# Three-branch attention with two more buffers and a longer pipeline, and the low part of softplus on VectorE

## Chip, cores and metric

The kernel runs on one core of a Trainium2 chip, as one program with one launch. The metric is the device time of that program in microseconds (us); lower is better. The median of three runs of the kernel before is 2275.87 us (2273.51 to 2281.44).

## What is computed

Two transformer blocks for one sequence of 512 tokens with 1024 channels. The first block has a hybrid mixer, a cross attention and a feed-forward part. The second has two layers. Its first layer is stick-breaking attention, its second is an attention with three branches, and each is followed by an MLP. Every weight matrix product is made three times, as high times high, low times high and high times low part, to keep float32 accuracy. The two places that the change touches are these, shortened from the reference:

```python
# stick-breaking attention, 16 heads of 64
z = einsum('bqhd,bshd->bhqs', q, k) * scale
causal = key_pos[None, :] < t[:, None]
log_1m = where(causal, log_sigmoid(-z), 0.0)          # -softplus(z)
excl = cumsum(log_1m, axis=3, reverse=True) - log_1m
a = where(causal, exp(log_sigmoid(z) + excl), 0.0)
o = einsum('bhqs,bshd->bqhd', a, v)

# attention with three branches: compressed keys, selected blocks, window; 16 heads in 4 groups
p_cmp = softmax(where(valid_c, q . k_cmp * scale, NEG))
p_sel = softmax(where(valid_s, q_rot . k_sel * scale, NEG))
p_w   = softmax(where(valid_w, q_rot . k_w * scale, NEG))
out   = sum over the branches of gate * (p @ v), then @ w_o
```

At 512 tokens the 8 key blocks are fewer than the 16 that would be selected, and the window holds all 512 tokens, so the second and third branch are both plain causal attention, with keys and values of their own.

## The kernel before

The program goes through seven stages (`PHASES`): mixer, cross attention, feed-forward, stick-breaking attention, MLP, three-branch attention, MLP. Weights stream in from HBM piece by piece. `Weights.hi` makes the high part of a piece on ScalarE (line 341) and `Weights.lo` its low part, tile `wl`, on VectorE (line 350). The program is scheduled by hand: each engine does its instructions in the order in which the Python code records them, and waits where one of them needs what is not there yet. So the two tables below set the work of every engine in the two stages.

**Stick-breaking attention** (`s_all`). The unit is a head, 16 in all. A step of the loop over `i` records the parts of `S_ORDER`, each for the unit that is its lag behind. Part `proj` makes the projection of a pair of heads (in even steps the queries, in odd steps the keys), 24 matmuls. `scores` makes z in PSUM. `evac` (tile `st`, line 1614) is the scaled copy of the projection. `cap` limits z to 30 into tile `sT` (lines 1662 and 1663, two instructions). `exp` makes Exp and Ln on ScalarE (1668, 1669), `soft` takes the maximum with z (1675, 1676). `high` runs on GpSimd: two small instructions and the high part `sph` of the softplus (1684, 1685, 1686). `low` is the difference `spl` of the softplus and its high part (1691), 128 x 1280, also on GpSimd. `weights` then adds the sums of both parts to the scores on TensorE. It has a lag of 1, so it stands behind the projection and the scores of the next unit. `low` has lag 1 as well and stands behind `scores` and ahead of `evac` and `cap` in the table.

**Three-branch attention** (`n_attend`). The work is cut into 4 groups of heads. A group has one unit for the compressed branch, called c unit below (methods `c_...`), and then 32 units (methods `n_...`): two pairs of heads, for each pair both other branches (b = 0 and 1), for each the two heads, and for each head four blocks of 128 queries in the order 3, 2, 0, 1, where block c has c + 1 blocks of keys. There are 132 units in all. The table `ORDER` says which part is recorded for which unit in iteration `i`: part with lag L works on unit i - L.

```python
ORDER = (("scores", 0), ("out", 7), ("head", 9), ("bias", 1), ("turn", 4), ("exp", 2),
         ("sums", 2), ("tick", 0), ("move", 5), ("scale", 2))
```

`scores` (TensorE) writes one of three PSUM banks. `bias` (VectorE, line 2055) adds the causal mask, scales and finds the row extreme, into a buffer `np` of which there are `NP`. `exp` (ScalarE, 2060) also sums the rows. `sums` (VectorE, 2064) takes the reciprocal. `scale` (GpSimd, 2069) multiplies by it and by the gate. `turn` (TensorE, 2077) transposes the probabilities into one of four PSUM banks. `move` copies them to SBUF, half on VectorE (2088), half on ScalarE (2090). `out` (TensorE) does the product with the values only after the last block of the second head of a pair, so in every eighth unit, with 16 matmuls. Where b is 0 four more go ahead of them, for the compressed branch (tile `cp`). `head` splits a finished pair of heads. For a c unit the same parts do more: `c_bias` has three VectorE instructions of 128 x 512, `c_sums` four, and `c_scale` (2162) one on GpSimd.

`tick` records one more instruction of each background generator. Here it is `g_query`, which rotates the queries of the next pair of heads: a shuffle on VectorE, six instructions on GpSimd, and then for each head a high part on ScalarE (2034), a low part on VectorE (2036) and a DMA of the result to the other half of the partitions (2039, tile `nq`). It is started in iteration 4 and 20 of a group (`QSTART`), and so its second, eighth and following instructions come in fixed iterations after that. `DRAIN` places the first matmuls of the output projection in the last iterations.

Of the kernel before, what the change touches and what calls it, by code (L numbers as in the profile page):

```python
# [10 lines left out]
F32 = mybir.dt.float32  # L11
# [3 lines left out]
ALU = mybir.AluOpType  # L15
# [15 lines left out]
PHASES = ("mix", "xattn", "ffn", "stick", "mlp1", "nsa", "mlp2")  # L31
BANKS = {"b": range(8), "bp": [0], "bo": [1], "za": [2, 3], "zb": [4, 6],
         "s": [0, 1, 2], "t": [3, 4, 5, 6], "av": [7], "f": [0, 1, 2, 3]}
NP = 6
FF_BLOCKS = ((0, 8), (8, 16), (16, 22))
SHUF = list(range(8, 16)) + list(range(0, 8)) + list(range(16, 32))

# [430 lines left out]
class Kernel:  # L468
# [1219 lines left out]

    def s_low(self, i):
        t, _, hi, lo, _, _ = self.hd[i]  # L1690
        self.nc.gpsimd.tensor_tensor(lo, t, hi.bitcast(F32), op=ALU.subtract)  # L1691

    def s_weights(self, i):

# [250 lines left out]
    def gate(self, gt):  # L1945
# [3 lines left out]
        for c in range(4):  # L1949
# [9 lines left out]

    QORD = (3, 2, 0, 1)  # L1960

    ORDER = (("scores", 0), ("out", 7), ("head", 9), ("bias", 1), ("turn", 4), ("exp", 2),
             ("sums", 2), ("tick", 0), ("move", 5), ("scale", 2))
    DRAIN, QSTART = 9, 4

    def n_attend(self):
        self.causal = self.wide("causal", self.ph, "causal")
# [17 lines left out]

        for i in range(n + max(lag for _, lag in self.ORDER) + 1):
            if i == n:
                lead = [(self.W.get(f"no{m}", 3 - m), self.bank("s")) for m in range(3)]
            for part, lag in self.ORDER:
                if part == "tick":  # L1990
# [11 lines left out]
        nxt, nx = self.next_norm() if self.nxt else None, self.newx() if self.nxt else None  # L2002
        self.back, self.fetched, self.back_tag = {}, 0, ("np", NP)
        self.fetch(2)
# [45 lines left out]
    def n_bias(self, u):  # L2050

        w = P * u["c"] + P
        p = u["p"] = self.tmp("np", bufs=NP)[:, :w]
        u["mx"] = self.tmp("nmx", (P, 1), bufs=8)
# [77 lines left out]
    def c_bias(self, u):  # L2132
        nc = self.nc
        p = u["p"] = self.tmp("np", bufs=NP)
        mask = self.cst("cmp_mask").rearrange("p (c n) -> p c n", c=4)
# [68 lines left out]
```

## Time and profile before

| what | value |
|---|---|
| median of three runs | 2275.87 us |
| the profiled execution | 2278.95 us |
| its span, first to last instruction | 2277.1 us |
| mean granted TensorE clock | 0.980 of full |
| TensorE busy | 2159.2 us (95%) |
| VectorE, ScalarE, GpSimd busy | 1230.7, 870.4, 494.5 us |
| stick-breaking units with `weights` waiting for GpSimd | 961 to 1128 us of the span |
| three-branch units | 1683 to 1863 us of the span |

TensorE is busy nearly all the time, and most of it is weight products back to back. The two stages of the change are the ones in which TensorE waits in a repeating pattern. They are read with the waits by engine, the timelines by engine, and busy time in stretches. A share of busy time over the whole span says little here.

### The profile page before, as it was taken

The numbers are of one execution on the slowest core, as the hardware profiler recorded it, in microseconds if no ns is written. First come the engines' busy times: TensorE is split into PE (matmuls) and PEld (weight loads), VectorE is DVE, ScalarE is ACT, GpSimd is POOL, SyncE is SP. The second block draws the span as 40 slices with busy tenths as digits, with TensorE's granted clock in tenths as the row PEclk, the third lists the DMA queues.
The fourth block names the chain that finished last, engine by engine and source line by source line (L and its number), as shares of the span: only waits on it lengthen the run. The fifth ranks groups of instructions, "written<-read, shape, count | busy, mean of one in ns | idle before, by whom it ended". The sixth has DMA issues, their size and how long they took to land.

```text
span 2277.1 us, 26704 instructions
## 1 busy us (share of the span) xinstructions
PE 2159.2 (95%) x10250; PEld 1750.3 (77%) x10250; DVE 1230.7 (54%) x1917; ACT 870.4 (38%) x1377; POOL 494.5 (22%) x495
## 2 busy tenths in 40 slices
PE   8899999999999999999899999998988889999998
PEld 5677788888888887777678888887775568888886
DVE  6998756454333435666545443446567755534333
ACT  4333434343222224355534232232446653523222
POOL 3333401111110104244410000023447651000001
PEclk9999999999999999999999999999999999999999
DMA  4122434122323222422133332332330113332231
GB/s 142 61 70 71 133 108 152 57 73 93 102 93 102 92 85 92 130 65 65 47 120 94 101 102 93 100 107 99 118 95 20 30 43 116 93 102 93 93 102 65
DMA packets 63376, 205.94 MB, mean 90 GB/s; under 512 B 7952, under 2 KB 8336, under 8 KB 63120
## 3 DMA queue, kind: packets, MB, share of 16 engines
q1 hardware_dynamic: 59504, 196.86, 27.6%
q10 hardware_dynamic: 3744, 7.37, 0.9%
q8 instruction: 80, 1.31, 0.2%
q14 instruction: 48, 0.39, 0.1%
HBM read 189.39 MB, written 6.29 MB: 86 GB/s over the span
## 4 chain that ended last, share of the span: by engine, by line
PE 74%; DVE 12%; POOL 5%; issue 4%; ACT 4%; DMA 0%; ACTq 0%; POOLq 0%; DVEq 0%; SPq 0%
PE psum L540 59%; PE b L540 12%; DVE wl L350 2%; PE psum L2077 1%; POOL spl L1691 1%; DVE t L908 1%; DVE pv L1089 1%; POOL np L2069 1%; POOL sph L1686 1%; POOL cx L1802 1%; DVE xl L553 1%; ACT xh L552 1%; ACT sT L1668 0%; ACT sT L1669 0%; DVE prev L1061 0%
## 5 line engine op out<-in xcount | busy, mean ns | idle before, releaser
L540 PE MATMUL psum<-xh,wh 128*128 128x512 f32 x1560 | 611.4, 392 | 1.0 <-DVE h L628 0.9
L540 PE MATMUL psum<-xh,wl 128*128 128x512 f32 x1560 | 608.6, 390 | 1.8 <-DVE wl L350 1.5
L540 PE MATMUL psum<-xl,wh 128*128 128x512 f32 x1560 | 608.5, 390 | 0.0
L341 ACT ACTIVATE wh<-ws 128x1024 fp32r<-128x1024 f32 (+1 forms) x346 | 356.3, 1038 | 388.9 <-PE psum L540 327.9
L350 DVE TENSOR_TENSOR wl<-ws,wh 128x1024 fp32r<-128x1024 f32 (+2 forms) x332 | 427.0, 1291 | 105.5 <-ACT wh L341 105.2
L540 PEld LDWEIGHTS psum<-xh,wl 128*128 128x128 f32 x1560 | 293.0, 188 | 66.1 <-DVE wl L350 4.3
L540 PEld LDWEIGHTS psum<-xh,wh 128*128 128x128 f32 x1560 | 293.3, 188 | 63.1 <-issue 3.0
L540 PEld LDWEIGHTS psum<-xl,wh 128*128 128x128 f32 x1560 | 293.3, 188 | 61.0 <-DVE xl L550 0.3
L540 PE MATMUL b<-xh,wh 128*128 128x512 f32 (+1 forms) x488 | 195.0, 400 | 8.5 <-ACT wh L341 6.7
L540 PE MATMUL b<-xh,wl 128*128 128x512 f32 (+1 forms) x488 | 192.6, 395 | 3.8 <-POOL wl L350 1.9
L540 PE MATMUL b<-xl,wh 128*128 128x512 f32 (+1 forms) x488 | 192.4, 394 | 0.5 <-DVE xl L553 0.5
L540 PE MATMUL psum<-hh,wh 128*128 128x512 f32 x320 | 125.1, 391 | 0.0
L540 PE MATMUL psum<-hh,wl 128*128 128x512 f32 x320 | 124.6, 389 | 0.0
L540 PE MATMUL psum<-hl,wh 128*128 128x512 f32 x320 | 124.6, 389 | 0.0
L1357 DVE TENSOR_TENSOR h<-h,psum 128x512 f32<-128x512 f32 x48 | 33.1, 689 | 161.2 <-PE psum L540 161.2
L540 PEld LDWEIGHTS b<-xh,wh 128*128 128x128 f32 (+1 forms) x488 | 92.5, 189 | 28.4 <-ACT wh L341 6.7
L1348 ACT ACTIVATE t<-t 128x512 f32<-128x512 f32 x64 | 40.5, 632 | 188.9 <-DVE t L1347 188.9
L540 PEld LDWEIGHTS b<-xh,wl 128*128 128x128 f32 (+1 forms) x488 | 92.0, 188 | 26.3 <-DVE wl L350 3.3
L553 DVE SCALAR_TENSOR_TENSOR xl<-h,cols,xh 128x512 fp32r<-128x512 f32 x64 | 76.6, 1213 | 61.8 <-ACT xh L552 61.8
L540 PEld LDWEIGHTS b<-xl,wh 128*128 128x128 f32 (+1 forms) x488 | 92.4, 189 | 20.4 <-DVE xl L553 1.2
L2069 POOL TENSOR_SCALAR np<-np,nsm,gates 128x512 f32<-128x512 f32 (+3 forms) x128 | 83.4, 654 | 46.8 <-DVE nsm L2064 34.1
L2077 PE MATMUL psum<-small,np 128*128 128x128 f32 x336 | 66.4, 302 | 27.2 <-POOL np L2069 19.1
(497 smaller groups left out, 3159.3 us busy)
## 6 DMA issues: line engine op xcount, KB each, us to landing
ws<-in_wst SPq DMA_DIRECT2D x332, 512.0 KB, 3.4
h<-in_xT SPq DMA_DIRECT2D x16, 256.0 KB, 3.7
kk<-kk SPq DMA_DIRECT2D x16, 256.0 KB, 3.3
nq<-nq SPq DMA_DIRECT2D x16, 256.0 KB, 2.9
ws<-in_wst SPq DMA_DIRECT2D x8, 384.0 KB, 3.1
spill<-back SPq DMA_DIRECT2D x8, 256.0 KB, 2.0
back<-spill ACTq DMA_DIRECT2D x8, 256.0 KB, 3.6
spill<-h ACTq DMA_DIRECT2D x8, 256.0 KB, 5.8
```

Of the source, the lines that this page charges most:

```text
L341: self.nc.scalar.activation(hi[:, :n], s, AF.Copy)
L350: e.tensor_tensor(lo[:, :n], s, hi[:, :n].bitcast(F32), op=ALU.subtract)
L540: self.nc.tensor.matmul(ps, a, b, start=start, stop=stop, skip_group_check=again)
L552: nc.scalar.activation(hi, src, AF.Copy, scale=scale)
L553: nc.vector.scalar_tensor_tensor(lo, src, scale, hi.bitcast(F32), op0=ALU.mult, op1=ALU.subtract)
L908: nc.vector.scalar_tensor_tensor(t, u[:, q:q + T], cw[:, q:q + 1], t, op0=ALU.mult, op1=ALU.add)
L1089: nc.vector.tensor_tensor(o[:, a:], src[:, a:], src[:, a - n:528 - n], op=ALU.add)
L1348: nc.scalar.activation(t, t, AF.Square)
L1357: nc.vector.tensor_tensor(self.h[:, m, :], self.h[:, m, :], ps, op=ALU.add)
L1686: self.nc.gpsimd.tensor_scalar(hi, t, 1.0, 0.0, op0=ALU.mult, op1=ALU.add)
L2069: self.nc.gpsimd.tensor_scalar(u["p"], u["p"], u.pop("sm"), self.gates[:, u["c"], e:e + 1], op0=ALU.mult, op1=ALU.mult)
L2077: self.nc.tensor.transpose(ps[:, s], p[:, s], self.ident)
```

## The change

Three edits. The low part of softplus is recorded on VectorE instead of GpSimd, at the same place of the stage's table. The buffers `np` go from 6 to 8. The table of the three-branch attention gets longer lags (turn 4 to 6, move 5 to 7, out 7 to 9, head 9 to 10, scale 2 to 4, sums 2 to 3) and another order within an iteration: `scale` right behind `sums`, `head` behind it, `tick` last. `DRAIN` follows.

```diff
-NP = 6
+NP = 8
...
     def s_low(self, i):
         t, _, hi, lo, _, _ = self.hd[i]
-        self.nc.gpsimd.tensor_tensor(lo, t, hi.bitcast(F32), op=ALU.subtract)
+        self.nc.vector.tensor_tensor(lo, t, hi.bitcast(F32), op=ALU.subtract)
...
-    ORDER = (("scores", 0), ("out", 7), ("head", 9), ("bias", 1), ("turn", 4), ("exp", 2),
-             ("sums", 2), ("tick", 0), ("move", 5), ("scale", 2))
-    DRAIN, QSTART = 9, 4
+    ORDER = (("scores", 0), ("out", 9), ("bias", 1), ("turn", 6), ("exp", 2), ("sums", 3),
+             ("scale", 4), ("head", 10), ("move", 7), ("tick", 0))
+    DRAIN, QSTART = 10, 4
```

How instructions stand on two engines, before and now. On VectorE, between two units of the stick-breaking stage (the number in a name counts tiles, `sT_6880` is the first unit's and `sT_6942` the second's):

```order
 L1676 TENSOR_TENSOR sT_6880<-sT_6880,psum 128x768
 L350 TENSOR_TENSOR wl_6899<-ws_6753,wh_6898 128x1024
+L1691 TENSOR_TENSOR spl_6894<-sT_6880,sph_6893 128x1280
 L1614 SCALAR_TENSOR_TENSOR st_6940<-psum,r_begin 128x512
 L1662 TENSOR_SCALAR sT_6942<-psum 128x512
```

The low part of one unit now stands in VectorE's queue ahead of the copy of the projection and the cap of the next unit. GpSimd's queue keeps the three instructions of `high` alone.

On TensorE, in the first group of the three-branch stage, where the second pair of heads begins. `nq_11664` is the second head of the first pair; the first head of the second pair is `nq_11848` before and `nq_11842` now; `cp` and `pt` are operands of `out`. Before:

```order
L540 MATMUL psum<-pt_11768,vs_10631 64x128
L540 MATMUL psum<-pt_11823,vs_10631 64x128
L2077 MATMUL psum<-small,np_11840 128x128
L540 MATMUL psum<-ks_10630,nq_11664 128x256 x2
L2077 MATMUL psum<-small,np_11854 128x128 x2
L540 MATMUL psum<-ks_10630,nq_11848 128x512 x2
L2077 MATMUL psum<-small,np_11869 128x128 x4
```

And now:

```order
L540 MATMUL psum<-ks_10630,nq_11664 128x256 x2
L2077 MATMUL psum<-small,np_11802 128x128 x4
L540 MATMUL psum<-ks_10630,nq_11664 128x256 x2
L2077 MATMUL psum<-small,np_11815 128x128 x3
L540 MATMUL psum<-ks_10630,nq_11842 128x512 x2
L540 MATMUL psum<-cp_11770,vc_11691 64x512 x2
L540 MATMUL psum<-pt_11785,vs_10631 64x512
```

Before, the long `out` was done two units ahead of the new head's first scores. Now it comes right behind them.

## Rows read from the trace of the kernel before

**Rows 1.** The page: busy time by engine; the chain that ended last, by engine.
```profile
PE 2159.2 (95%) x10250; PEld 1750.3 (77%) x10250; DVE 1230.7 (54%) x1917; ACT 870.4 (38%) x1377; POOL 494.5 (22%) x495
...
PE 74%; DVE 12%; POOL 5%; issue 4%; ACT 4%; DMA 0%; ACTq 0%; POOLq 0%; DVEq 0%; SPq 0%
```

**Rows 2.** Waits, stick-breaking stage (950 to 1145): waiter, releaser: total, times, longest.
```profile
PE psum L540 <- POOL spl L1691: 17.4, 9, 3.1
```

**Rows 3.** Timeline of TensorE, first matmul on spl: start, us, what [idle before].
```profile
964.74 0.69 PE L540 MATMUL psum<-spl,none 128*128 128x384 f32 x1 [2.91 <-POOL spl L1691]
987.82 0.44 PE L540 MATMUL psum<-spl,none 128*128 128x384 f32 x1 [1.83 <-POOL spl L1691]
1011.42 0.44 PE L540 MATMUL psum<-spl,none 128*128 128x384 f32 x1 [1.84 <-POOL spl L1691]
...
1127.73 0.44 PE L540 MATMUL psum<-spl,none 128*128 128x384 f32 x1 [3.15 <-POOL spl L1691]
```

**Rows 4.** Timeline of GpSimd, one pair of units, and spl of the first and 15th.
```profile
961.41 3.27 POOL L1691 TENSOR_TENSOR spl<-sT,sph 128x1280 fp32r<-128x1280 f32 x1
1006.24 2.13 POOL L1686 TENSOR_SCALAR sph<-sT 128x1280 fp32r<-128x1280 f32 x1
1008.45 2.91 POOL L1691 TENSOR_TENSOR spl<-sT,sph 128x1280 fp32r<-128x1280 f32 x1
1015.72 1.26 POOL L1686 TENSOR_SCALAR sph<-sT 128x1280 fp32r<-128x1280 f32 x1
1017.06 2.95 POOL L1691 TENSOR_TENSOR spl<-sT,sph 128x1280 fp32r<-128x1280 f32 x1
...
1123.94 3.73 POOL L1691 TENSOR_TENSOR spl<-sT,sph 128x1280 fp32r<-128x1280 f32 x1
```

**Rows 5.** Timeline of VectorE, the same pair of units, and a wl alone.
```profile
999.90 0.96 DVE L1663 TENSOR_SCALAR sT<-psum 128x768 f32<-128x768 f32 x1 [0.30 <-PE psum L540]
1005.70 1.53 DVE L350 TENSOR_TENSOR wl<-ws,wh 128x1024 fp32r<-128x1024 f32 x1 [0.58 <-ACT wh L341]
1007.75 0.69 DVE L1614 SCALAR_TENSOR_TENSOR st<-psum,r_begin 128x512 f32<-128x512 f32 x1 [0.51 <-PE psum L540]
1008.40 0.69 DVE L1662 TENSOR_SCALAR sT<-psum 128x512 f32<-128x512 f32 x1
...
1017.78 3.32 DVE L350 TENSOR_TENSOR wl<-ws,wh 128x1024 fp32r<-128x1024 f32 x1 [3.17 <-ACT wh L341]
...
1152.07 1.23 DVE L350 TENSOR_TENSOR wl<-ws,wh 128x1024 fp32r<-128x1024 f32 x1 [2.49 <-ACT wh L341]
```

**Rows 6.** Waits, three-branch stage (1690 to 1863), columns as in rows 2.
```profile
DVE nsm L2064 <- ACT np L2060: 21.6, 46, 1.9
...
PE psum L2077 <- POOL np L2069: 18.9, 34, 2.9
...
PE psum L2077 <- POOL np L2162: 7.9, 4, 2.2
```

**Rows 7.** Stretches: us, busy PE, PEld, DVE, ACT, POOL, granted clock, DMA.
```profile
1733.00:1755.00 22.00, 18.84 (x114) 13.04 (x114) 15.69 (x66) 15.35 (x46) 16.00 (x24) 0.92 0.11 25
1755.00:1777.00 22.00, 18.19 (x123) 12.79 (x122) 16.90 (x66) 14.33 (x43) 14.71 (x24) 1.00 0.12 27
```

**Rows 8.** Timeline of TensorE: turn of two c units; out of one pair and the next head.
```profile
1734.28 1.11 PE L2077 MATMUL psum<-small,np 128*128 128x128 f32 x4 [1.89 <-POOL np L2162]
...
1748.00 1.08 PE L540 MATMUL psum<-cp,vc 128*64 128x512 f32 x4
...
1751.70 0.71 PE L540 MATMUL psum<-ks,nq 128*128 128x512 f32 x2
...
1777.79 0.83 PE L2077 MATMUL psum<-small,np 128*128 128x128 f32 x4 [1.89 <-POOL np L2162]
```

**Rows 9.** VectorE's low part of that head; its DMA, from issue to landing.
```profile
1747.01 0.68 DVE L2036 TENSOR_TENSOR nq<-qr,nq 64x512 fp32r<-64x512 f32 x1
...
DMA to landing us min/median/max: 2.8/2.9/4.4
```

## The prediction

> **What bounds the kernel now.** The page comes first: TensorE is busy 95% of the span, and 74% of the chain that ended last lies on it [rows 1]. So only what TensorE waits for, or what makes it slower, can give time back. The waits by engine then say where it waits. In the stick-breaking stage it is one thing: nine waits for the low part `spl`, 17.4 us in all [rows 2]. Of these the first unit has 2.91 and the 15th 3.15 us, and the 11 us that are left are six waits like the two shown, 1.83 to 1.84 us, one in every pair of units [rows 3]. A pair takes 1011.42 - 987.82 = 23.6 us. In the three-branch stage TensorE waits for GpSimd's `scale`: 18.9 us in 34 waits on ordinary units and 7.9 us in four waits on c units, 26.8 us together [rows 6]. The c units stand 1777.79 - 1734.28 = 43.5 us apart, which is one group [rows 8].
>
> Is any engine full there? In 44 us of a group TensorE is busy 18.84 + 18.19 = 37.0 us, and VectorE 15.69 + 16.90 = 32.6 us [rows 7]. None is. TensorE's clock is 0.92 in one of the two stretches: 0.08 x 22 = 1.8 us of clock lost per group. The slow stretch begins behind a wait of 1.89 us for a c unit [rows 7, 8], so I count part of that loss to the waits. Without waits and at full clock TensorE would need 37.0 - 1.8 = 35.2 us per group. VectorE comes close behind it, with 32.6 / 33 = 0.99 us per unit. The stage is bound by the latency from one engine to the next, with two engines nearly full beneath it.
>
> **Term 1: low part on VectorE.** It removes 16 GpSimd instructions of 2.91 to 3.73 us [rows 4] and adds 16 on VectorE. No row shows that one there. The nearest are the same subtraction on 1024 columns, 1.23 us alone, and a 512-column instruction, 0.69 us [rows 5]. The slope gives 1.23 + 256 x 0.54 / 512 = 1.50 us for 1280. The upper bound is the same subtraction when disturbed: `wl` took 3.32 us when it began inside a GpSimd `spl` [rows 4, 5], so 3.32 x 1.25 = 4.1 us. I take 1.50, as GpSimd has nothing left to do behind `sph` until the next unit.
>
> The new wait is on VectorE. `spl` waits for `sph`, and behind it stand `st` and both caps of the next unit. That closes a loop that was not there: cap, Exp and Ln, maximum, `sph`, `spl`, `st`, cap of the next unit. From the second cap to the start of `spl` it is 1008.45 - 999.90 = 8.55 us [rows 4, 5]. Then `spl` 1.50, `st` 0.65 and the first cap 0.65 (start to start, 1008.40 - 1007.75): 11.35 us per unit, 22.7 per pair. Before it was 23.6, so a pair saves 0.9 us, and six pairs 5.4. What is late next is this loop, no longer GpSimd.
>
> In 8.55 `sph` counts at 2.13 us. The other unit of the pair had it at 1.26 [rows 4], with no `wl` beside it. With 1.26 there the pair would be 21.8 us, and TensorE's own work is 23.6 - 1.84 = 21.8, so a pair saves at most 1.8 and six 10.8. I take the smaller saving: the odd unit's chain now starts later, behind `spl`, and its `sph` comes to lie beside the `wl` of 1017.78. The Trainium skill (SBUF, section "Who interferes with whom") says that a VectorE instruction with two SBUF inputs and a GpSimd instruction that reads SBUF exclude each other for a whole instruction. The trace agrees: 3.32 is 1.23 plus about what was left of the running `spl`. By that rule both units stand at 2.13 and six pairs save 5.4; by the undisturbed row 10.8.
>
> The first unit's wait shrinks by 3.27 - 1.50 = 1.8 us, and the 15th's by 3.73 - 1.50 = 2.2. The DMAs of the keys come about 2 us later in a step and have a projection of 24 matmuls to hide behind: nothing. Term 1 is 5.4 + 1.8 + 2.2 = **9 us**, between 4 (the pairs gain nothing) and 15.
>
> **Term 2: the longer pipeline.** No instruction is added or removed. Before, the transposes of a unit follow its reciprocal by two iterations, and that reciprocal waits in the same iteration for Exp: 46 such waits on VectorE, 21.6 us [rows 6]. TensorE can thus be about one unit ahead of VectorE. When it comes to an `out` it leaves VectorE about one unit of work and then issues no scores for 2 to 3 us (an `out` with its `cp` begins at 1748.00, and the new head's scores, the second ones behind it, at 1751.70 [rows 8]). VectorE runs dry, and TensorE later waits for what VectorE did not do. Now the transposes follow the reciprocal by three iterations, and Exp has an iteration to itself. The lead grows to about two units, so each of the 16 `out`s costs one unit less: 16 x 0.99 = 15.8 us. Eight buffers are what the two extra iterations need: with six, bias would take a buffer in the iteration in which it is transposed. They do nothing else.
>
> For the c unit the compressed branch gets two iterations more, and an `out` now falls in its iteration. Of four waits (7.9 us) I leave 1 us each: 4 us gained, bounds 0 and 7.9.
>
> Against this stands a transfer. The low part of the next pair's first head comes in iteration 13, now at its end, and its scores in iteration 17. Before, the low part began at 1747.01 and the scores at 1751.70, with an `out` between; the DMA takes 2.9 us [rows 8, 9]. Now that `out` stands behind the scores. TensorE is one to two units ahead, so it arrives two units or one, 2.0 or 1.0 us, after the low part, and waits 1.0 to 2.0 us. I take 1.5 in each of four groups: 6 us lost, bounds 0 and 3.0 each, or 12. The even pairs have the c unit between and lose nothing.
>
> The clock: 1.8 us per group, 7 us in all. About half of the waits go, so I take half of that, 3.5.
>
> Term 2 is 15.8 + 4 - 6 + 3.5 = **17 us**, between a loss of 4 (half of the lead's gain, no other gain, 12 lost to the transfer) and (43.5 - 35.2) x 4 = 33 (TensorE never waits). A group should take about 39 us. The extra iteration at the end only drains, beside the output projection's first matmuls: nothing.
>
> **Sum.** 9.4 + 17.3 is 27 us. The profiled execution took 2278.95, so 2252; it lies 3.1 us above the median, so the median becomes 2275.87 - 27 = 2249 us.
>
> **Rivals.**
> - *The waits only move.* VectorE at 0.99 us per unit is close to TensorE, and the transfer waits its full 2.9 us. Then term 2 is 8 - 12 = -4, term 1 stays 9: 2271. For it speaks that the two engines are busy 37.0 and 32.6 of 44 us [rows 7]; against it that the 26.8 us of waits come from units whose chain gets two more iterations. Chance 0.08.
> - *Slower: `spl` disturbed on VectorE.* If it takes 4.1 us, the loop is 8.55 + 4.1 + 1.3 = 13.95 us and a pair 27.9: six pairs lose 25.8, first and 15th unit 1.2. With term 2 the time is 2275.87 + 27 - 17 = 2286. It decides from 11.8 - 9.85 = 1.95 us on. Against it: the disturbance in the rows needs a GpSimd instruction at the same time, and none is left there. Chance 0.04. The same section of the Trainium skill asks for such a partner too.
> - *TensorE becomes the only bound.* Both terms at their upper ends, 15 + 33: 2228. For it speaks that the new lags take every direct wait apart; against it the transfer and VectorE's 32.6 us. Chance 0.07.
> - *The change does not do what it says*, as the added buffers push something else: the order on the engines shows both moves, so 0.01.
>
> **How the numbers follow.** The forecast has 0.80, and its bounds are 4 - 4 and 15 + 33 us gained, both terms seldom at one end. The range from 2230 (46 us gained) to 2268 (8 us) leaves out those ends and with them the second rival and most of the first and third, under 0.2 in all. About 7 us, 0.3% of the time, is what a measurement of this kernel can tell from no change. Faster than 2269: forecast 0.80, third rival 0.07 and a part of the first, together 0.90. Within 0.3%: 0.06. Slower: 0.04.
>
> **What would show it.** Right: waits of TensorE on `spl` near 1 us per pair, now with VectorE as releaser, `spl` at 1.5 us, pairs 22.7 us apart; c units about 39 us apart; waits on `scale` below 15 us in all; a new TensorE wait of 1 to 2 us ahead of the third head's first scores in each group. Wrong: `spl` above 1.95 us, pairs at 23.6 us or more, or groups still at 43 us.

## The result and the profile after

| what | before | after |
|---|---|---|
| median | 2274.73 us (four runs, 2273.51 to 2281.44) | 2252.02 us (four runs, 2250.17 to 2254.06) |
| ratio, 95% interval | | 0.9894 [0.9872, 0.9917] |
| span of the profiled execution | 2277.1 us | 2250.8 us |
| mean granted TensorE clock | 0.980 | 0.986 |
| stick-breaking stage, with the weight product behind it | 233.70 us | 224.34 us |
| next stretch, up to the three-branch stage | 479.75 us | 475.33 us |
| three-branch stage | 260.85 us | 247.62 us |
| TensorE busy in the stick-breaking stage (1087 matmuls) | 212.44 us | 210.86 us |
| TensorE busy in the next stretch (some 2086 matmuls) | 467.51 us | 462.93 us |
| TensorE busy in the three-branch stage (1281 matmuls) | 230.03 us | 224.14 us |

The change is faster by 1.1% (0.8 to 1.3%), and 2252 lies 3 us above the forecast. By the ratio it gained 24 us, where 27 were forecast. The stages are cut at the same instruction in both traces. Term 1 came to 233.70 - 224.34 = 9.4 us (forecast 9.4), term 2 to 260.85 - 247.62 = 13.2 us (forecast 17.3). Of the 4.4 us of the stretch between them about 3.4 belong to one execution and not to the change; experiment 8 shows it.

What a stage lost is idle time of TensorE or busy time. Its matmuls are the same in both kernels, so less busy time for them goes with the granted clock. Term 1 is 7.8 us of idle time (21.3 to 13.5) and 1.6 us of busy time, at a clock of 0.98 before and 0.99 now. Term 2 is 7.3 us of idle time (30.8 to 23.5) and 5.9 us of busy time, at 0.94 and 0.97.

**The page of the changed kernel**, busy time by engine and the chain by engine [rows 1]:

```profile
PE 2148.9 (95%) x10250; PEld 1740.8 (77%) x10250; DVE 1228.7 (55%) x1933; ACT 864.4 (38%) x1377; POOL 449.0 (20%) x479
...
PE 71%; DVE 14%; ACT 5%; POOL 5%; issue 4%; DMA 1%; ACTq 0%; POOLq 0%; DVEq 0%; SPq 0%
```

Sixteen instructions went from GpSimd to VectorE, and yet VectorE is busy 2 us less than before (1228.0 us in experiment 1, where they alone moved): most of the 23.9 us it took over it got back from its own instructions beside GpSimd. From 940 to 1150 the mean `wl` went from 2.12 to 1.34 us, and the low parts of the keys (`kk`) from 17.9 to 9.5 us in all. Of the chain 3% has gone from TensorE and 2% to VectorE.

**Stick-breaking stage.** Waits of TensorE, 940 to 1145, columns as in [rows 2]:

```profile
PE psum L540 <- DVE spl L1691: 7.0, 9, 1.1
PE psum L540 <- POOL sph L1686: 2.4, 2, 1.3
PE psum L540 <- ACT sA L1717: 1.8, 2, 1.3
```

The 17.4 us of [rows 2] are now 7.0 us, with VectorE as releaser. The second and third line are partly new: 2.4 instead of 1.3, and 1.8 instead of nothing. Where the time came from is read from the first matmul on `spl` of each unit, on the timeline of TensorE [rows 3]:

```profile
963.73 0.69 PE L540 MATMUL psum<-spl,none 128*128 128x384 f32 x1 [1.08 <-DVE spl L1691]
...
985.79 0.45 PE L540 MATMUL psum<-spl,none 128*128 128x384 f32 x1 [1.09 <-DVE spl L1691]
...
1030.47 0.45 PE L540 MATMUL psum<-spl,none 128*128 128x384 f32 x1 [0.58 <-DVE spl L1691]
...
1052.83 0.45 PE L540 MATMUL psum<-spl,none 128*128 128x384 f32 x1 [0.58 <-DVE spl L1691]
...
1097.49 0.44 PE L540 MATMUL psum<-spl,none 128*128 128x384 f32 x1 [0.57 <-DVE spl L1691]
1108.02 0.44 PE L540 MATMUL psum<-spl,none 128*128 128x384 f32 x1 [1.09 <-DVE spl L1691]
1118.49 0.45 PE L540 MATMUL psum<-spl,none 128*128 128x384 f32 x1 [0.82 <-DVE spl L1691]
```

A pair takes 1052.83 - 1030.47 = 22.4 us; it was 23.6. TensorE still waits 0.57 us in each. The rest of a pair is then 21.8 us, TensorE's own work as worked out before. What it waits for is the new loop, and it stands whole on the chain of work that ended last (start, us, what), here for one unit:

```profile
1040.19 1.49 DVE spl L1691
1041.68 0.60 DVE st L1614
1042.28 0.60 DVE sT L1662
1042.88 0.88 DVE sT L1663
...
1043.84 1.28 ACT sT L1668
...
1045.15 1.28 ACT sT L1669
...
1047.06 0.96 DVE sT L1676
...
1049.12 2.14 POOL sph L1686
...
1051.28 0.81 DVE spl L1691
```

From one `spl` to the next it is 1051.28 - 1040.19 = 11.1 us; 11.35 was forecast. In [rows 4] one unit of a pair had `sph` at 2.13 us and the other at 1.26. Here are two units in a row, on GpSimd's timeline, and the `wl` beside them on VectorE's:

```profile
1049.12 2.13 POOL L1686 TENSOR_SCALAR sph<-sT 128x1280 fp32r<-128x1280 f32 x1
...
1060.20 2.30 POOL L1686 TENSOR_SCALAR sph<-sT 128x1280 fp32r<-128x1280 f32 x1
```

```profile
1048.58 1.53 DVE L350 TENSOR_TENSOR wl<-ws,wh 128x1024 fp32r<-128x1024 f32 x1 [0.58 <-ACT wh L341]
1051.28 1.49 DVE L1691 TENSOR_TENSOR spl<-sT,sph 128x1280 fp32r<-128x1280 f32 x1 [1.17 <-POOL sph L1686]
...
1060.15 1.22 DVE L350 TENSOR_TENSOR wl<-ws,wh 128x1024 fp32r<-128x1024 f32 x1 [1.07 <-ACT wh L341]
1062.54 1.49 DVE L1691 TENSOR_TENSOR spl<-sT,sph 128x1280 fp32r<-128x1280 f32 x1 [1.16 <-POOL sph L1686]
```

Both units are now disturbed by a `wl`. Take the second: `sph` begins at 1060.20 and `wl` runs until 1061.37, so 1.17 us of it are left; 1.26 + 1.17 = 2.43, and the row has 2.30. `spl` itself has 1.49 us in all 16 units, and `wl` no longer has its 3.32 us of [rows 5].

**Three-branch stage.** Waits of TensorE, 1670 to 1850 [rows 6], then of VectorE, and of VectorE in the kernel before (1690 to 1863):

```profile
PE psum L540 <- DVE nmx L2055: 8.6, 18, 1.3
PE psum L540 <- DMA nq<-nq: 6.3, 4, 1.6
PE psum L2077 <- POOL np L2069: 5.0, 8, 1.6
PE psum L2077 <- POOL np L2162: 1.1, 3, 0.4
```

```profile
DVE np L2055 <- PE psum L540: 17.7, 9, 3.0
DVE ol L550 <- ACT oh L549: 10.6, 7, 1.7
...
DVE nsm L2064 <- ACT np L2060: 1.6, 4, 0.4
```

```profile
DVE np L2055 <- PE psum L540: 10.7, 13, 2.0
DVE ol L550 <- ACT oh L549: 5.7, 4, 1.9
```

The waits on `scale` fell from 18.9 to 5.0 us, those on the c unit from 7.9 to 1.1, and the 46 waits of VectorE on Exp from 21.6 to 1.6. Two lines are new. TensorE's scores wait for `bias` (8.6 us; before it was a single wait of 1.4 us, at the start of the stage), and the third head of each of the four groups waits for its transfer (6.3 us). In all it is 21.0 us instead of 26.8 + 1.4 = 28.2. VectorE still runs dry at `out`: it has nine waits of up to 3.0 us on the scores, and seven in `head` (`ol`) on ScalarE, which needs the result of an `out`. So of the 20 us that it no longer waits for Exp, 12 have moved to these two lines (10.7 to 17.7 and 5.7 to 10.6). Start times on TensorE's timeline, of two late transfers [rows 8]:

```profile
1732.33 0.70 PE L540 MATMUL psum<-ks,nq 128*128 128x512 f32 x2 [1.59 <-DMA nq<-nq]
...
1773.39 0.70 PE L540 MATMUL psum<-ks,nq 128*128 128x512 f32 x2 [1.58 <-DMA nq<-nq]
```

A group takes 1773.39 - 1732.33 = 41.1 us, and the c units stand as far apart (1719.09 and 1760.15). It was 43.5, and 39 was forecast. The last view is busy time in stretches of about a group, over the whole stage (columns as in [rows 7]). Of the kernel before:

```profile
1690.00:1733.00 43.00, 37.13 (x220) 27.03 (x220) 30.40 (x127) 29.26 (x87) 30.13 (x46) 0.89 0.12 26
1733.00:1777.00 44.00, 37.02 (x236) 25.83 (x236) 32.59 (x131) 29.68 (x88) 30.72 (x47) 0.96 0.12 26
1777.00:1820.00 43.00, 38.22 (x232) 26.24 (x232) 29.74 (x123) 28.27 (x85) 29.54 (x46) 0.92 0.12 26
1820.00:1863.00 43.00, 34.35 (x214) 23.15 (x214) 29.58 (x124) 29.26 (x88) 29.05 (x41) 0.96 0.10 26
```

And of the changed one:

```profile
1678.00:1720.00 42.00, 36.94 (x228) 26.71 (x228) 32.09 (x129) 28.43 (x88) 30.65 (x48) 0.94 0.12 27
1720.00:1761.00 41.00, 35.94 (x237) 24.80 (x237) 31.97 (x130) 28.82 (x88) 29.62 (x47) 1.00 0.13 28
1761.00:1802.00 41.00, 35.96 (x238) 24.81 (x237) 31.98 (x130) 28.81 (x88) 29.63 (x47) 1.00 0.13 28
1802.00:1840.00 38.00, 33.53 (x210) 22.77 (x209) 24.93 (x107) 25.53 (x78) 25.29 (x38) 0.96 0.15 43
```

Look at the granted clock, third column from the end. Before, it costs 0.11 x 43 + 0.04 x 44 + 0.08 x 43 + 0.04 x 43 = 11.6 us, now 0.06 x 42 + 0.04 x 38 = 4.0 us. The difference, 7.6 us, counts a low clock as lost even where TensorE waits, so it is an upper estimate. By the busy time of the table it is 5.9 us, and with 28.2 - 21.0 = 7.2 us of waits that gives 13.1 of the 13.2 us of the stage.

### The profile page after: what moved, and what is told of

The parts are those of the page before. It is cut to its first block, busy times and chain, and to the rows that moved or that the text cites. A ratio compares the mean times of both kernels' runs of the same rounds, so it can differ in the third digit from the quotient of the medians.

```text
span 2250.8 us, 26731 instructions
## 1 busy us (share of the span) xinstructions
PE 2148.9 (95%) x10250; PEld 1740.8 (77%) x10250; DVE 1228.7 (55%) x1933; ACT 864.4 (38%) x1377; POOL 449.0 (20%) x479
## 4 chain that ended last, share of the span: by engine, by line
PE 71%; DVE 14%; ACT 5%; POOL 5%; issue 4%; DMA 1%; ACTq 0%; POOLq 0%; DVEq 0%; SPq 0%
PE psum L540 56%; PE b L540 13%; DVE wl L350 2%; POOL sph L1686 1%; ACT sT L1668 1%; ACT sT L1669 1%; DVE t L908 1%; PE psum L2077 1%; DVE spl L1691 1%; DVE pv L1089 1%; POOL cx L1802 1%; DVE xl L553 1%; DVE sT L1663 1%; DVE np L2055 1%; ACT xh L552 1%
## 5 line engine op out<-in xcount | busy, mean ns | idle before, releaser
L350 DVE TENSOR_TENSOR wl<-ws,wh 128x1024 fp32r<-128x1024 f32 (+2 forms) x332 | 414.6, 1254 | 91.8 <-ACT wh L341 91.5
L1347 DVE SCALAR_TENSOR_TENSOR t<-psum,r_mlp 128x512 f32<-128x512 f32 x64 | 44.1, 689 | 79.2 <-PE psum L540 79.1
```

Source lines behind the costliest of these rows:

```text
L350: e.tensor_tensor(lo[:, :n], s, hi[:, :n].bitcast(F32), op=ALU.subtract)
L1347: nc.vector.scalar_tensor_tensor(t, ps, 0.0, norm.bc, op0=ALU.max, op1=ALU.mult)
```

## The experiments

Ratios are against runs of the kernel before that were taken with each experiment on the same chip. Stage times are cut as above. The change to the three-branch table is tested as a whole: no run here separates the longer lags from the new order within an iteration.

**1. The low part on VectorE alone** (the kernel before with this line):

```diff
-        self.nc.gpsimd.tensor_tensor(lo, t, hi.bitcast(F32), op=ALU.subtract)
+        self.nc.vector.tensor_tensor(lo, t, hi.bitcast(F32), op=ALU.subtract)
```

> The kernel before with the low part of softplus on VectorE and nothing else. Theory (two independent terms): the stick-breaking stage alone gets shorter, by the 9 us of term 1, pairs of units 22.3 to 22.7 us instead of 23.6; about 2266 us where the kernel before takes 2275; the three-branch groups stay at 43.5 us. Rival (the gain of the whole change lies in the longer pipeline, and the stick-breaking stage only looks shorter in one profile): within 3 us of the kernel before.

Measured: 2266.21 us against 2276.48, ratio 0.9949 [0.9933, 0.9964]. The stick-breaking stage takes 224.68 us, the three-branch stage stays at 259.83. Term 1 is real, and it lies where it was put: 9.0 us of the stick-breaking stage.

**2. The pipeline alone** (the changed kernel with that line put back):

```diff
-        self.nc.vector.tensor_tensor(lo, t, hi.bitcast(F32), op=ALU.subtract)
+        self.nc.gpsimd.tensor_tensor(lo, t, hi.bitcast(F32), op=ALU.subtract)
```

> The change with the low part of softplus left on GpSimd: eight buffers and the new table alone. Theory: the three-branch stage takes 13 us less (groups 41 instead of 43.5 us), the stick-breaking stage is as before (pairs 23.6 us, TensorE waits 17 us for spl); about 2262 us. Rival (the two parts overlap, each gives most of the 23 us alone): below 2257 us.

Measured: 2266.49 us, ratio 0.9948 [0.9933, 0.9964]; stick-breaking 233.74, three-branch 247.76 us. Its waits, 940 to 1145:

```profile
PE psum L540 <- POOL spl L1691: 17.4, 9, 3.1
```

This is the line of [rows 2] to the digit. The product of the two ratios is 0.9897, the whole change has 0.9894: the parts don't touch each other.

**3. Eight buffers alone:**

```diff
-NP = 6
+NP = 8
```

> The kernel before with eight buffers np instead of six, old table. Theory (the buffers only make room for the longer lags; with the old lags no unit ever waits for one): same as before, within 3 us, groups at 43.5 us. It is also a second execution of the old order: if the 4 us that the changed kernel's profile shows less between the two stages come from the granted clock of one execution and not from the change, this profile can show them too (clock 1.00 instead of 0.88 to 0.94 in that stretch). Rival (the extra buffers free bias earlier): 5 us or more faster.

Measured: 2276.62 us, ratio 0.9999 [0.9989, 1.0008], ten runs. The buffers do nothing by themselves.

**4. The changed kernel with six buffers:**

```diff
-NP = 8
+NP = 6
```

> The changed kernel with six buffers np instead of eight. Theory: bias now takes the buffer of the unit that is transposed in the iteration before its own, and that transpose stands behind an out in every eighth unit; VectorE then waits for TensorE through each out, about one unit (1 us) for each of 16 outs: 8 to 16 us slower than the changed kernel, so 2260 to 2268, with waits of bias on L2077 in the profile. Rival (six buffers are enough, since bias is held up by the scores anyway): within 3 us of the changed kernel, 2252.

Measured: 2264.2 us, ratio 0.9941 [0.9921, 0.9961]; three-branch 257.70 us, 10.1 more than with eight. The wait of VectorE, 1670 to 1850:

```profile
DVE np L2055 <- PE psum L2077: 32.3, 13, 5.2
```

`bias` waits for the transposes to give a buffer back, 13 times, up to 5.2 us. So the new table needs the buffers, and with six it keeps only 260.85 - 257.70 = 3.2 of its 13.2 us.

**5 and 6. The query's rotation two iterations earlier, and two later:**

```diff
-    DRAIN, QSTART = 10, 4
+    DRAIN, QSTART = 10, 2
```

(and 6 in the other one.)

> The changed kernel with QSTART 2 instead of 4: the background work on the next queries starts two iterations earlier, so the DMA of a pair's first head is issued two iterations earlier, with the same instructions. Theory (the transfer that the longer lags uncover holds the three-branch stage at 41 instead of 39 us a group): the four TensorE waits on the DMA, 6.3 us in the changed kernel, are gone and groups take 1.5 us less; about 2246 us. Rival (VectorE is the bound by then, and its waits take over): no more than 2 us less than the changed kernel, with the waits of TensorE on bias or scale longer by what the DMA waits lose.

> The changed kernel with QSTART 6 instead of 4: the same DMA two iterations later. Theory: TensorE arrives at the new head's scores when the DMA has just begun, and each of the four waits grows by about the two units, 2 us, to 3 to 4 us: about 8 us slower than the changed kernel, 2260. Rival (the wait is filled with work that other engines need anyway): within 3 us of the changed kernel.

Measured, earlier: 2258.27 us, ratio 0.9908 [0.9886, 0.9929]; three-branch 248.45 us. The waits of TensorE in its three-branch stage:

```profile
PE psum L540 <- DVE nmx L2055: 15.2, 13, 1.4
PE psum L2077 <- POOL np L2069: 7.3, 15, 1.6
```

The transfer is never waited for any more, as it should be, but nothing is gained. The 6.3 us turned up again on `bias` and `scale`, 22.5 us in all against 21.0. Here my theory missed and the rival held.

Later: 2268.84 us, ratio 0.9954 [0.9938, 0.997]; three-branch 261.42 us, 13.8 more. Its line on the transfer, same view:

```profile
PE psum L540 <- DMA nq<-nq: 13.7, 4, 3.5
```

The wait grew from 6.3 to 13.7 us, by 7.4, and the stage by almost twice that, and by more than the 8 us expected. TensorE idles 8.4 us more in it and is busy 5.4 us longer (229.50 us) with the same 1281 matmuls. In the first three stretches (cut as above) the granted clock is 0.84, 0.92 and 0.92, where the changed kernel has 0.94, 1.00 and 1.00. So the time of the transfer counts when it becomes longer and not when it vanishes.

**7. The low part behind the cap.** The place of the instruction in VectorE's queue:

```diff
-    S_ORDER = (("proj", 0), ("scores", 0), ("low", 1), ("evac", 0), ("cap", 0),
+    S_ORDER = (("proj", 0), ("scores", 0), ("evac", 0), ("cap", 0), ("low", 1),
```

> The changed kernel with the part low behind cap in the table of the stick-breaking stage instead of ahead of evac: on VectorE the low part of a unit then stands behind st and both caps of the next. Theory (the place in VectorE's queue sets the stage; ahead of the caps it closes a loop of 11.2 us per unit, behind them it waits for the scores instead): the low part cannot start before the second cap ends, about 1 us behind the scores, and TensorE waits 2 to 2.5 us for it in every unit instead of 0.6 in every second: pairs of units about 26 us instead of 22.3, about 25 us slower than the changed kernel, 2277. Rival (the chain through GpSimd sets the stage and the place matters little): within 5 us of the changed kernel.

Measured: 2292.36 us, ratio 1.0061 [1.0037, 1.0086]; stick-breaking 262.14 us, 37.8 more than the changed kernel. The waits of its stick-breaking stage, and four stretches of it:

```profile
PE psum L540 <- DVE spl L1691: 31.7, 15, 3.3
```

```profile
990.00:1030.00 40.00, 35.55 (x170) 26.86 (x170) 17.96 (x22) 15.86 (x19) 6.06 (x9) 0.89 0.25 66
1030.00:1070.00 40.00, 33.33 (x163) 26.49 (x163) 24.42 (x27) 19.07 (x22) 6.08 (x9) 0.91 0.16 42
1070.00:1110.00 40.00, 33.33 (x169) 24.69 (x168) 22.92 (x26) 18.12 (x21) 6.06 (x9) 0.91 0.22 64
1110.00:1150.00 40.00, 32.21 (x154) 25.50 (x155) 24.19 (x29) 20.99 (x27) 6.07 (x9) 0.87 0.14 40
```

The loop of the changed kernel is opened: `spl` hardly waits for `sph`. In its place `spl` waits behind the cap of the next unit, which needs that unit's scores, and TensorE, done with them, waits 2.2 us for `spl` and its weights in nearly every unit. That is 31.7 - 7.0 = 24.7 us more on `spl`, as expected, and 21.0 us more idle time in all, since other waits went. The clock, which the expectation left out, adds the rest: it is 1.00 in the changed kernel from 990 to 1150, and here 0.87 to 0.91, and the same 1087 matmuls keep TensorE busy for 227.64 us instead of 210.86, 16.8 us more. So the place of one instruction in one queue decides whether the whole change makes the kernel 1.1% faster or 0.6% slower.

**8. The changed kernel once more**, without an edit:

> The changed kernel once more, for a second profile and beside the three others. Theory: the 4 us that its first profile shows less in the stretch between the two changed stages belong to the granted clock of that one execution; here that stretch takes 478 to 480 us as in the other profiles, and the two changed stages take 224 and 248 us again. Rival (the change shortens that stretch too): about 475 us again.

Measured: 2256.07 us, ratio 0.9902 [0.9881, 0.9922]; stick-breaking 224.40, three-branch 247.96 us, and the stretch between them 478.8 instead of 475.33 us. One view of that stretch in this execution:

```profile
1603.00:1657.00 54.00, 50.69 (x236) 40.32 (x237) 26.34 (x37) 17.94 (x25) 16.24 (x23) 0.94 0.31 98
```

The granted clock is 0.94 there. In the first profile of the same kernel it was 1.00 (1601 to 1654), in the kernel before 0.91 (1610 to 1667), with the same instructions in all three. Over all traces the stretch takes 479.7 to 480.0 us in the three kernels with `low` on GpSimd, 478.6 to 478.9 in the ten other traces with it on VectorE, and 475.33 in that first profile alone. So 3.4 us belong to the execution. The other 1.0 us goes with the move of `low`; by which way is not shown. The parts of the gain are then 9.4 + 13.2 + 1.0 = 23.6 us, and the ratio gives 24.

**9 to 12. Attempts at a better table.** Three edits: `head` one iteration later (with `DRAIN`), the earlier rotation of experiment 5 with it, and a fourth PSUM bank for the scores, taken from the transposes.

```diff
-              ("scale", 4), ("head", 10), ("move", 7), ("tick", 0))
-    DRAIN, QSTART = 10, 4
+              ("scale", 4), ("head", 11), ("move", 7), ("tick", 0))
+    DRAIN, QSTART = 11, 4
...
-          "s": [0, 1, 2], "t": [3, 4, 5, 6], "av": [7], "f": [0, 1, 2, 3]}
+          "s": [0, 1, 2, 3], "t": [4, 5, 6], "av": [7], "f": [0, 1, 2, 3]}
```

> The changed kernel with head one iteration later (lag 11 instead of 10, and DRAIN 11): it no longer stands in the iteration right behind its out. Theory (the new table put a wait on VectorE: seven low parts of head wait 10.6 us for ScalarE, which waits for the out; before it was 5.7 us in four): that wait goes, VectorE gains up to 1.5 us at each of seven, about 5 us faster than the changed kernel. Rival (VectorE would wait for scores in that time anyway, since TensorE is in the out): within 3 us of the changed kernel.

> Both: head one iteration later and the next queries two iterations earlier (QSTART 2). Theory (the early queries gained nothing since VectorE was the next to be late): with VectorE's wait gone as well the two together give more than each alone, 5 to 9 us faster than the changed kernel. Rival: within 3 us of it, the waits of TensorE on bias taking the place.

> As the one before, and four PSUM banks for scores with three for transposes instead of three and four. Theory (VectorE runs dry in each out because TensorE can be no more than the scores' banks ahead; it is the lead that counts): one more unit of lead gives VectorE up to 0.8 us more work in each of 16 outs, 8 to 13 us on top of the two other edits, groups at 37 to 38 us. Rival (three banks for transposes hold TensorE up by as much): no faster than without it, with waits of L2077 on L2088 and L2090 in the profile.

> The changed kernel with four banks for scores and three for transposes alone. Theory: as above, the lead alone, 5 to 10 us faster than the changed kernel, the waits of TensorE on bias (8.6 us) gone. Rival: within 3 us of it, since the wait for the DMA stops TensorE at the same place.

| kernel | median, us | ratio | TensorE waits: bias, scale, c unit, transfer, move (us) | sum |
|---|---|---|---|---|
| changed kernel | 2252.02 | 0.9894 [0.9872, 0.9917] | 8.6, 5.0, 1.1, 6.3, 0 | 21.0 |
| 5, earlier rotation | 2258.27 | 0.9908 [0.9886, 0.9929] | 15.2, 7.3, 0, 0, 0 | 22.5 |
| 9, `head` later | 2254.44 | 0.9897 [0.9878, 0.9917] | 9.8, 4.3, 1.1, 6.3, 0 | 21.5 |
| 10, both | 2263.22 | 0.9929 [0.9906, 0.9952] | 18.1, 8.1, 0, 0, 0 | 26.2 |
| 11, both, fourth bank | 2256.56 | 0.9899 [0.9878, 0.992] | 0, 11.2, 1.9, 0, 11.8 | 24.9 |
| 12, fourth bank alone | 2255.83 | 0.9899 [0.9882, 0.9917] | 0, 8.6, 5.5, 7.8, 0.2 | 22.1 |

None beats the changed kernel, so all four theories missed the gain they named; 9, 11 and 12 equal it within their intervals, and 10 is slower than 9 by 8.8 us on the same chip. Read along the rows: each edit does take away the wait it aims at. The later `head` of 9 takes most of VectorE's waits in it (10.6 us fall to 1.6, without one of 8.7 us at the end of the stage), but its waits on the scores grow instead, from 17.7 to 24.3 us. The fourth bank takes all of the waits on `bias`, so those come from the three score banks. It does not keep VectorE from running dry: its waits on the scores are 19.7 us in 12, against 17.7. With the bank gone from the transposes, TensorE waits as long for `scale`, the c unit and the transfer instead, or for the copies of `move`:

```profile
PE psum L2077 <- POOL np L2069: 11.2, 22, 1.7
PE psum L2077 <- DVE pt L2088: 5.9, 5, 1.4
```

(from experiment 11). Four banks for each was not tried: the table of banks gives out all eight, and `out` needs its own. Experiment 10 loses its time in the three-branch stage: 257.74 us against 247.32 in 9, of which 5.0 are idle time of TensorE and 5.4 busy time, at a granted clock of 0.95 against 0.98. Why the two edits together cause waits that neither causes alone stays open.

## Why the prediction was right, and which of its steps were off

**Term 1: the sum right, its parts shifted.** The first matmuls on `spl` of both traces divide the 9.4 us. That the sum came out to the digit is partly luck: it held no clock, and 1.6 of the 9.4 us are TensorE's busy time and not waits.
- First unit: 10.8 us from the stage's start before, 8.9 now: 1.8 us, as forecast.
- The pairs: from the first of these matmuls to the one 12 units on, 1105.80 - 964.74 = 141.1 us before and 1097.49 - 963.73 = 133.8 now. That is 7.3 us for six pairs, 5.4 were forecast. The price of `spl` (1.50, measured 1.49) and of both `sph` (2.13; 2.13 and 2.30) was right. Two of these loops were worked out as 22.7 us and took 1062.54 - 1040.19 = 22.35; the loop was sized 0.2 us per unit too long. The Trainium skill's rule (SBUF — State Buffer, section "Who interferes with whom") chose rightly between the two rows for `sph`: both units are disturbed.
- The 15th unit: forecast 2.2 us, got 0.2. This step failed. The wait of 3.15 us [rows 3] is down to 0.82, but the two units ahead of it wait more than before: 1.09 on `spl`, 1.1 on `sph` and 1.3 on `sA` (L1717). There TensorE has no weight matmuls ahead of the 14th unit's sums and only 6 and 12 ahead of the 15th's (1110.2 to 1111.8 and 1114.5 to 1117.3 of its timeline), where a projection has 24, and the loop of 10.5 us per unit shows bare. In all the waits behind the 13th unit's sums rose from 4.6 to 5.7 us. That the stretch still gained 0.2 us goes with the clock, 0.96 from 1070 to 1110 before and 1.00 now. I had priced one wait there by the duration of `spl` and not asked what the new loop costs a unit without cover.

**Term 2: 13.2 instead of 17.3.** By the rows of the result:

| step | forecast | measured |
|---|---|---|
| lead of TensorE over VectorE | +15.8 | 18.9 + 1.4 - 5.0 - 8.6 = +6.7 |
| c unit | +4 | 7.9 - 1.1 = +6.8 |
| transfer of `nq` | -6 | -6.3 |
| clock (TensorE's busy time) | +3.5 | 230.03 - 224.14 = +5.9 |
| sum | 17.3 | 13.1 (stage: 13.2) |

The step that was mis-sized is the lead. The waits on `scale` did fall by 13.9 us, near the 15.8. But I counted a lead of two units without asking where two units of scores would stand. With three banks TensorE comes to wait for `bias` to free one: 8.6 us in 18 waits. That these waits come from the banks experiment 12 shows, where the fourth bank removes just these. It does not show that the banks hold the gain of the lead down: with these waits gone the sum is 22.1 us and the time the same. The reckoning of one unit for each `out` failed before that, since VectorE still runs dry there. Part of it was made up by the c units (6.8 us for 4) and by the clock (5.9 for 3.5): I let half of the loss come back, and in the two middle groups all of it came back (0.96 and 0.92 before, 1.00 now).

The transfer was forecast by its mechanism and size: four waits of 1.6 us, ahead of the third head's scores in each group, 1.5 taken. But its meaning was off. Experiment 5 removed it and gained nothing; it is one of several waits of which only the sum counts, as long as it isn't the longest.

**The rivals.** *The waits only move* is refuted as a whole, since term 2 gained 13.2 us, but it describes well what is left: in the table of experiments 5 and 9 to 12 the sum of waits stays between 21 and 26 us. *`spl` disturbed* did not come about (1.49 us in all 16), yet its direction has been seen: experiment 7, with `spl` at 1.48 us and at another place in the queue, is slower than before. It was the place that had to be right and not only the duration. *TensorE the only bound* fell with the 21.0 us of waits. *The change does not do what it says* fell with experiments 1 and 2, where each part gives its own gain. What limits a group to 41 us is not settled. VectorE, busy 32 of 41 us, runs dry at `out` and must catch up behind it; that fits all six rows of the table, but no run here changed VectorE's work in this stage.

## What to carry to other kernels

When an instruction moves to another engine, write down the loop that its place in the new queue closes (here `spl` to `spl`, 11.1 us), and look for the units that have least other work to hide it. Longer lags need a place for every unit that is in flight: count the buffers of each kind (here `np`, six against eight, 10 us; then the score banks, 8.6 us of new waits) before the gain. But a wait that an edit removes is a gain only if no other takes its place: experiments 5, 9 and 12 each removed a wait and gained nothing. Price a wait together with the clock: in the three-branch stage TensorE's busy time fell by 5.9 us with the granted clock, its waits by 7.2 us.

## What the runs showed of the hardware

- The same subtraction of 128 x 1280 takes 1.49 us on VectorE in all 16 units, and 2.91 to 3.73 on GpSimd [rows 4].
- `wl` on VectorE (two inputs in SBUF) and an instruction of GpSimd stretch each other by nearly what is left of the one that runs: `sph` has 1.26 us alone and 2.13 to 2.30 beside a `wl`. So the move gave VectorE no more busy time in all (1230.7 us before, 1228.0 in experiment 1, 1228.7 after).
- The granted clock of the same instructions differs between executions of one kernel: 1.00 and 0.94 in the view of experiment 8, in a stretch that took 475.3 and 478.8 us. A difference of that size in one profile is no evidence of a change.
- Longer waits went with a lower granted clock, so that a stage grew by more than they did: in experiment 6 TensorE idles 8.4 us more and the stage takes 13.8 us more, at a granted clock of 0.92 instead of 1.00 in the middle groups. In experiment 7 it is 21.0 and 37.8 us, at 0.87 to 0.91 instead of 1.00.
